# Weight sums in three stretches, each addition a round behind its copy; token tiles behind weight loads; two more gate buffers

## The chip, the cores and the metric

The kernel runs on one core of one Trainium2 chip. The metric is the device time of one launch in microseconds. The core has five engines with one instruction stream each (TensorE or PE, VectorE or DVE, ScalarE or ACT, GpSimd or POOL, SyncE or SP), and 16 DMA engines, to which here SP hands work through hardware queues and POOL through a software queue. Each stream runs in order: an instruction that waits holds back all that stands behind it on its engine.

## The reference

One step of a hybrid decoder layer over 1024 prompt tokens and 8 sample tokens, all in fp32. One input projection feeds two head groups, and one output projection joins them.

```python
p = project(rmsnorm(xp, norm_w[l]), w_in[l], b_igate[l], b_fgate[l])   # h @ w_in, split column-wise
att = dsa_prompt(p['q'], p['k'], p['v'], p['qi'], p['ki'], p['wi'])    # indexer scores, top-k keys, attention
h_ml, C1, n1, m1 = mlstm_run(p['mq'], p['mk'], p['mv'], p['ig'], p['lf'], zC, zn, zm, ML_CHUNK)
xp = merge(xp, att, p, h_ml, ml_norm_w[l], w_out[l])   # gates, then x + concat([a, mo]) @ w_out
# the sample tokens: the same with a paged cache (cache_k, cache_v, cache_idx_k) and given mLSTM states
```

The model width is 2048. The tokens are handled as 1032 columns (1024 and 8) in two halves of 516. This case turns on the wide columns of `w_in`: 40 tiles of 128 columns (the mLSTM q, k, v, its output gate and both SiLU gates).

## The kernel before

**Matmuls.** Each fp32 product is made of three matmuls on split operands. A raw tile is cast on ACT into a high part H, DVE subtracts H from the raw tile to leave a low part L, and PE adds H·H, H·L and L·H. A weight is used only after its load (SP), its cast (L262, or L1770 in the wide stage) and its subtraction (L263, or L1771).

**Stages on PE.** First come projection tiles 0 to 20 with the plain scheme (`proj`, matmuls at L1599), until about 522 us. Then `gate_stage` makes the 40 wide tiles in pairs by a seven-product scheme of the Strassen kind: of a pair of column tiles and the two token halves it forms sums of weight blocks and sums of token blocks, and needs fewer products for it. It has 140 products of 48 matmuls (L1782), until about 1607 us: first kinds 4 and 6 in turn (40 products, raw weights), then kind 1 (20), kind 3 (20), kind 2 (20), and at last kinds 0 and 7 in turn (40). The output projection (L2086 and L2153) follows.

**Weight sums.** Kinds 1, 3 and 2 read sums of two or more weight blocks, which lie in `usD[n, i]` in DRAM (n is the sum, i one of NP = 20 tile pairs; `b11` to `b22` are the four blocks of a pair). `job_usum` makes one sum of 512 KB by two DMAs: a copy of one block into place (`copy`, L1472 on SP for n = 0 and 3, L1474 on POOL for n = 1 and 2), and an accumulating DMA (`plus`, L1478 on POOL). There are 160 of these steps. A plus waits until its copy has landed, and so does a copy whose source is another sum.

**Token sums.** `xsD` holds sums of token tiles. `fill` (L1738) loads tiles of them, 258 KB each, into the buffers `xL` of a slot that a later kind reads; three ticks later they are split as weights are (L1731, L1733). A tick is half a product.

**Partial products.** PE's results go through DVE (`combine`, L1877) into buffers of 516 columns called `ev`, from there to DRAM (`put`, L1805, into `spD`), and are read back (`get`, L1801, from `spD` into an `ev` buffer) a product kind later. `outs` is the ring of four such buffers, which `get`, `put` and the gates share. `ones` are two buffers of that size, the halves of the tile `rstd`, which only the last stage uses after the reciprocal norms have been read from them.

**What sets the order.** A scheduler orders every engine's stream at build time by a simulation of the kernel; `tc.high_priority()` lets an instruction go ahead, `pin` keeps it in place, and `tc.issue_after(x)` puts it behind the instruction `x` on its queue. `pace["dma"]` is the last weight load that was written. Side jobs (indexer, attention on both token sets, mLSTM, the weight sums) run in three `Lane`s: each job has a first and a last time in units of a projection tile (T_AK = 9, T_G = 21 is the first wide tile, the wide stage goes to 61) and a number of steps, and its lane spreads the steps over that time. The lane of the sums runs beside the two others and gives its DMAs to the same SP and POOL streams. On POOL stand also the gathers of the paged index keys (`kp`, L1013, indirect DMAs), which feed matmuls on PE at L1035; the gathers for the sampled tokens' attention (`ck`, L1290); and on DVE that attention's products and sums (L1347, L1351). The selection of keys runs on ACT and DVE (L524, L548 to L553) and, for the sample tokens, through a count on PE (L1073) between DVE steps (L1069, L1090 to L1102).

Of the kernel before, what the change touches and what calls it, by code (L numbers as in the profile page):

```python
# [8 lines left out]
F32 = mybir.dt.float32  # L9
# [33 lines left out]
T_AK = 9  # L43
T_AV = 11
T_AQ = 13
T_G = 21
# [10 lines left out]
NP = (NT - T_G) // 2  # L57
# [120 lines left out]
def body(tc, A, stop=None):  # L178
    nc = tc.nc
    V, SC, G, PE, SY = nc.vector, nc.scalar, nc.gpsimd, nc.tensor, nc.sync  # L180
# [25 lines left out]
    early = ExitStack()  # L206
# [14 lines left out]
    pin = tc.keep_in_program_order  # L221
    pace = {}
# [5 lines left out]
    def dt_(shape, name):  # L228
        return tc.dram_tile(shape, F32, name=name)
# [15 lines left out]
    usD = dt_([4, NP, 128, 2, 4, 128], "usD")  # L245
# [1212 lines left out]
                yield 1  # L1458

    sums = set()  # L1460
    NE = 64

    def job_usum():
        def parts(i):
            c1 = T_G + 2 * i - 1
            return [[A["wa"][c, y] for y in range(2)] for c in (c1, c1 + 1)]

        def copy(n, i, src, queue):
            with tc.high_priority():
                if queue is SY:  # L1470
                    with tc.issue_after(pace["dma"]):
                        SY.dma_start(usD[n, i], src)  # L1472
                else:
                    pin(queue.dma_start(usD[n, i], src))  # L1474

        def plus(n, i, src):
            with tc.high_priority():
                pin(G.dma_start(usD[n, i], src, accum_op=OP.add, max_dma_last_dim=8192))  # L1478
            sums.add((n, i))

        for i in range(NP + 1):
            (b11, _), (b12, _) = parts(min(i, NP - 1))
            b22 = parts(i - 1)[1][1] if i else None
            if i < NP:
                copy(0, i, b11, SY)
                yield 1
            if i:
                copy(1, i - 1, usD[0, i - 1], G)
                yield 1
            if i < NP:  # L1490
                plus(0, i, b12)
                yield 1
            if i:
                plus(1, i - 1, b22)
                yield 1
        for n, src in ((3, None), (2, 1)):
            for i in range(NP):
                (_, b21), (b12, b22) = parts(i)
                copy(n, i, b22 if n == 3 else usD[1, i], SY if n == 3 else G)
                yield 1  # L1500
                plus(n, i, b12 if n == 3 else b21)
                yield 1

    def att_free():
        return "datt" in lanes[1].done and "k" in mlc
# [17 lines left out]

    groups = ((2, 3), (4, 5), (6, 7))

    def shares(gen, n):
        g = gen()

        def part(n):
            for _ in range(n):  # L1530
                w = next(g, 0)
                if not w:
                    return
                yield w
        return lambda: part(n), lambda: part(10 ** 6)

    sums_a, sums_b = shares(job_usum, NE)
    lanes = [Lane([Job("gates", 5, T_AK - 0.5, 12500, job_gates),
                   Job("index", T_AK + 1.5, 31.5, 6000 + sum(map(ix_weight, groups)), lambda: job_index(groups)),
                   Job("att", T_G + 17.6, 49.3, 2 * 2 * sum(2 * (1 + (i + 1) * 0.5) for i in range(8)) + 18, job_att, att_free),  # L1540
# [4 lines left out]
                   Job("qrows", T_G + 0.2, 27, 1, job_qrows),  # L1545
                   Job("datt", T_G + 9.2, 38.4, 10000 + 8 * 7000 + 34000 + 5 * 2500 + 8000 + 8000 + 5000, job_datt),
                   Job("dml", T_G + 20, 55.5, 28000 + 16 * 2500 + 5000, job_dml, hi_done)]),
             Lane([Job("early sums", T_AK + 2.5, 22.0, NE, sums_a),
                   Job("late sums", T_AK, 46.0, 8 * NP - NE, sums_b)])]
    gateV = gateS.rearrange("(k p) r -> k p r", p=128)  # L1550
    mixb = [None] * KT
    first = []
# [129 lines left out]
    def gate_stage():  # L1682
# [3 lines left out]
        raws, ones = [[one[:, 0], one[:, 1], one]], []  # L1686
        evs = evp.big["ev"].rearrange("p a b -> p (a b)")
        outs = [evs[:, x * HR:x * HR + HR].rearrange("p (c t) -> p c t", c=2) for x in range(4)]
        mlc["k"] = [X[:, 14:16, HR:HR + 512] for X in (XH, XL)]
        turn = {"raw": 0, "w": 0, "ev": 0, "one": 0, "n": 0}  # L1690
# [30 lines left out]
        def tick():  # L1721
            nonlocal pa0, pb0
            now = 4.0 * T_G + state["u"] * amount
            for lane in lanes:
                lane.step(now, amount)
            state["u"] += 1
            if splits and splits[0][0] <= state["u"]:
                _, h, l = splits.pop(0)
                with tc.high_priority():
                    with tc.issue_after(pace["act"]):  # L1730
                        SC.copy(h, l.bitcast(F32))  # L1731
                    with tc.issue_after(pace["dve"]):
                        V.tensor_tensor(l, l.bitcast(F32), h.bitcast(F32), OP.subtract)  # L1733
            if fills:
                f = fills.pop(0)
                if f:
                    h, l, src = f
                    SY.dma_start(l.bitcast(F32), src)  # L1738
                    splits.append((state["u"] + 3, h, l))
            if now >= 4.0 * T_PRE and pb0 is None:  # L1740
                lanes[0].ensure("ml")
                pb0 = mctx.enter_context(tc.tile_pool(name="pb0", bufs=1, side="right"))
            if now >= 4.0 * T_PA and pa0 is None:
                lanes[1].ensure("dml")
                pa0 = mctx.enter_context(tc.tile_pool(name="pa0", bufs=1, side="right"))
            while ready and ready[0][0] < state["u"] and (pb0 if ready[0][1] > 1 else pa0) is not None:
                pend.append(ready.pop(0)[1])
            for _ in range(2):
                if len(mids) > 4:
                    mixmake(*mids.pop(0), True)  # L1750
                if pend:
                    k = pend.pop(0)
                    mids.append(mixload(k, pb0 if k > 1 else pa0, True, G))
# [149 lines left out]
                mlc["lo"] = True  # L1903
        del extra, both
        ones += [rstd[:, c * HR:c * HR + HR].rearrange("p (c t) -> p c t", c=2) for c in range(2)]
        turn["p"] = 0

        def two():
            return [take("p", pj), take("p", pj)]
# [29 lines left out]
        def flush():  # L1939
            while muls:  # L1940
                times, ks = muls.pop(0)
                times()
                ready.extend((state["u"], k) for k in ks)
# [27 lines left out]
        def out_weight(q):  # L1971
            H, L, load, cast = wload(A["wo"][0, q], 128, wst, 2, 3)
            pin(load(slice(0, 4)))
            for x in cast(slice(0, 4)):
                pin(x)
            first.append((H, L))

        def last():
# [1 line left out]
            out_weight(2)  # L1980

        flush()
        for p in range(3):
            fetch(p)
        for p, (z, i, y) in enumerate(order):
# [9 lines left out]
            e, g = fetched.pop(p)  # L1995
# [93 lines left out]
    parts = [[(0, 0), (0, 1), (0, 2), (1, 0), (1, 1), (1, 2), (0, 3)], [(1, 3)]]  # L2089
# [38 lines left out]
    turn = [0]  # L2128
# [76 lines left out]
    late = []  # L2205
# [91 lines left out]
    for n in range(2):  # L2297
        p6, p4 = banks3(0), banks3(1)
        for k in range(8):
            with tc.high_priority():  # L2300
                b12 = wblock(0, 2 + n, k, pt, 6)
                b11 = wblock(0, n, k, pt, 6)
                b22 = wblock(1, 2 + n, k, pt, 6)
                b21 = wblock(1, n, k, wst, 2)
# [22 lines left out]
    for n in range(2):  # L2327
        ps = banks3(n)
        for k in range(8):
            with tc.high_priority():  # L2330
                b22 = wblock(1, 2 + n, k, pt, 6)
                b12 = wblock(0, 2 + n, k, *((wst, 2) if k % 2 else (pt, 6)))
# [133 lines left out]
```

## Time and profile before

| | us |
|---|---|
| median of 3 runs | 1963.96 (1962.99 to 1965.94) |
| the profiled run | 1964.0 |
| its span | 1962.2 |
| PE busy in it | 1895.3 |
| DVE busy | 1406.0 |
| ACT busy | 914.1 |
| POOL busy | 533.7 |

The profiled run is one execution, and the rows below come from it; what lies outside its span is 1.8 us. PE is busy for 97% of the span, so little is idle there (some 67 us). The questions are therefore where PE stands still, what it waits for there, and at which clock it runs next to these places. A row of the timeline gives the start, the duration, the engine, the line, the operation and its tiles, and in brackets the idle time before it with what ended that time. A row of the waits gives the total, the number of times and the longest. A row of the windows gives each engine's busy time in a stretch, then the granted clock of PE, the busy share of the DMA engines and the GB/s they moved.

### The profile page before, as it was taken

The page shows a single profiled execution, that of the slowest core. Times are in us where ns is not written, and L with a number is a line of the kernel's source. Part 1 is how long each engine was busy: PE and PEld are TensorE (multiplying, and loading weights), DVE is VectorE, ACT ScalarE, POOL GpSimd, SP SyncE. Part 2 cuts the span into 40 slices and gives each one's busy share as a digit, 9 for nine tenths or more (in the row PEclk, how much of TensorE's full clock was granted, in tenths as well). Part 3 has the DMA queues.
Part 4 walks back from the last instruction along what each step waited for, and adds up shares of the span by engine and source line. Part 5 has one row for each costly group of instructions (what it writes and reads, how often), then busy time and mean ns, then how long its engine had stood idle before and what let it go on. Part 6 is the DMA issues. An engine that isn't in the chain of part 4 may idle for free. (4 is left out here: it accounts for less than half of the span.)

```text
span 1962.2 us, 37412 instructions
## 1 busy us (share of the span) xinstructions
PE 1895.3 (97%) x13422; PEld 1820.9 (93%) x13422; DVE 1406.0 (72%) x3261; ACT 914.1 (47%) x1826; POOL 533.7 (27%) x614
## 2 busy tenths in 40 slices
PE   9999998999989999998899999999999989999997
PEld 9999998999979999998799999999999989977776
DVE  8554664767789985897465566657979866787797
ACT  8222252334543557621245565454656634454645
POOL 0599853321100001035111000001211340107632
PEclk9999998999989999999999999999999999999999
DMA  7577767879878759979998874458988778898866
GB/s 258 158 233 217 236 203 223 246 210 228 242 227 246 197 166 270 339 244 266 310 304 239 243 214 143 133 177 294 328 286 294 222 192 269 273 339 300 277 200 220
DMA packets 252918, 474.46 MB, mean 242 GB/s; under 512 B 40549, under 2 KB 116133, under 8 KB 246333
## 3 DMA queue, kind: packets, MB, share of 16 engines
q1 hardware_dynamic: 217261, 356.70, 55.8%
q0 software_dynamic: 21504, 107.32, 21.9%
q10 hardware_dynamic: 13968, 8.06, 1.4%
q8 instruction: 105, 1.72, 0.4%
q14 instruction: 80, 0.66, 0.1%
HBM read 381.54 MB, written 174.32 MB: 283 GB/s over the span
## 5 line engine op out<-in xcount | busy, mean ns | idle before, releaser
L1782 PE MATMUL pj<-xH 128*128 128x258 f32 x1920 | 548.2, 286 | 21.4 <-DVE ev L1877 14.1
L1782 PE MATMUL pj<-xL,xH 128*128 128x258 f32 x1920 | 548.2, 286 | 0.0
L1782 PE MATMUL pj<-xH,xL 128*128 128x258 f32 x1920 | 547.2, 286 | 0.0
L1782 PEld LDWEIGHTS pj<-xH 128*128 128x128 f32 x1920 | 365.2, 190 | 25.3 <-DVE ev L1877 15.3
L1782 PEld LDWEIGHTS pj<-xL,xH 128*128 128x128 f32 x1920 | 365.6, 190 | 2.4 <-issue 0.8
L1782 PEld LDWEIGHTS pj<-xH,xL 128*128 128x128 f32 x1920 | 365.4, 191 | 1.7
L1599 PE MATMUL pj<-xH,wH 128*128 128x344 f32 (+1 forms) x816 | 265.0, 328 | 1.9 <-DVE ev L385 1.1
L1599 PE MATMUL pj<-xL,wH 128*128 128x344 f32 (+1 forms) x816 | 266.2, 326 | 0.0
L1599 PE MATMUL pj<-xH,wL 128*128 128x344 f32 (+1 forms) x816 | 265.4, 326 | 0.0
L263 DVE TENSOR_TENSOR wL<-wraw,wH 128x512 fp32r<-128x512 f32 (+2 forms) x151 | 117.4, 789 | 106.2 <-ACT wH L262 99.9
L1478 POOL DMA_DIRECT2D usD<-in_wa_dram x80 | 66.5, 863 | 428.4 <-DMA usD<-in_wa_dram 228.8
L262 ACT CAST wH<-wraw 128x512 fp32r<-128x512 f32 (+2 forms) x151 | 89.8, 607 | 199.9 <-PE pj L1599 98.3
L1599 PEld LDWEIGHTS pj<-xH,wH 128*128 128x128 f32 x816 | 153.9, 189 | 3.6 <-DVE ev L385 1.8
L1599 PEld LDWEIGHTS pj<-xL,wH 128*128 128x128 f32 x816 | 154.1, 189 | 0.6 <-DVE xL L320 0.3
L1599 PEld LDWEIGHTS pj<-xH,wL 128*128 128x128 f32 x816 | 154.2, 189 | 0.4 <-DVE wL L263 0.3
L1770 ACT CAST xH<-wL 128x1024 fp32r<-128x1024 f32 (+1 forms) x91 | 76.1, 836 | 125.5 <-PE pj L1782 69.8
L1770 ACT CAST xH<-wH 128x1024 fp32r<-128x1024 f32 x91 | 76.0, 836 | 124.4 <-PE pj L1782 72.9
L2153 PE MATMUL pj<-wH,sH 128*128 128x512 f32 x336 | 131.3, 391 | 1.7 <-ACT wH L2137 1.7
L2153 PE MATMUL pj<-wH,sL 128*128 128x512 f32 x336 | 130.7, 390 | 0.0
L2153 PE MATMUL pj<-wL,sH 128*128 128x512 f32 x336 | 125.9, 393 | 4.8 <-DVE wL L2142 4.8
L477 ACT ACTIVATE rl<-bank 128x512 f32<-128x512 f32 (+2 forms) x160 | 79.8, 523 | 99.7 <-PE bank L475 55.1
L480 DVE SCALAR_TENSOR_TENSOR s<-rl,wiN,s 128x512 f32<-128x512 f32 (+2 forms) x150 | 106.6, 729 | 19.5 <-ACT rl L477 16.6
(492 smaller groups left out, 4507.4 us busy)
## 6 DMA issues: line engine op xcount, KB each, us to landing
usD<-in_wa_dram POOLq DMA_DIRECT2D x80, 512.0 KB, 7.8
wraw<-in_wt_dram SPq DMA_DIRECT2D x144, 256.0 KB
usD<-in_wa_dram SPq DMA_DIRECT2D x40, 512.0 KB
usD<-usD POOLq DMA_DIRECT2D x40, 512.0 KB, 7.2
wraw<-in_wa_dram SPq DMA_DIRECT2D x78, 256.0 KB
wraw<-in_wo_dram SPq DMA_DIRECT2D x64, 256.0 KB
ev<-spD SPq DMA_DIRECT2D x62, 258.0 KB
spD<-ev SPq DMA_DIRECT2D x60, 258.0 KB
```

Source lines behind the costliest of these rows:

```text
L262: a = SC.copy(H[:, s, :cols], raw[:, s, :cols])
L263: return a, V.tensor_tensor(L[:, s, :cols], raw[:, s, :cols], H[:, s, :cols].bitcast(F32), OP.subtract)
L477: SC.activation(r[:, :cn], p[:, :cn], AF.Relu)
L480: v = V.scalar_tensor_tensor(s[:, c0:c0 + cn], r[:, :cn], wv, s[:, c0:c0 + cn], OP.mult, OP.add)
L1478: pin(G.dma_start(usD[n, i], src, accum_op=OP.add, max_dma_last_dim=8192))
L1599: m = PE.matmul(ps[:cols, :cn], w_[:, k, :cols], x_[kk][:, c0:c0 + cn], start=(kk == ends[0] and z == 0), stop=(kk == ends[1] and z == 2))
L1770: paced("act", SC.copy(H[:, q], r))
L1782: PE.matmul(ps[c], w_[:, q, ks], x[y][:, c * CS:c * CS + CS], start=(first and q == 0 and k == 0 and z == 0), stop=(q == 1 and k == 3 and ...
L2153: PE.matmul(ps[b], S_[x][:, b * 128:b * 128 + 128], T_[y], start=(k == 0 and z == 0), stop=(k == 7 and z == 2))
```

## The change

1. `job_usum` writes each addition a round behind its copy. For n = 0 and 1 a round is now copy(0, i), copy(1, i-2), plus(0, i-1), plus(1, i-3); before, it was copy(0, i), copy(1, i-1), plus(0, i), plus(1, i-1). For n = 3 and 2 it is copy(i), plus(i-1); before, copy(i), plus(i).
2. The sums run in three stretches, not two. Before: 64 steps from tile 11.5 to 22, and 96 from there to 46. Now: 56 steps from tile 11.5 to 20.4, 62 from 22.4 to 33.2, and the last 42 from 38.8 to 47.
3. The loads of token sums (`xL<-xsD`) are queued behind the last weight load that was written before them.
4. The two halves of `rstd` join the ring of `ev` buffers for the 60 products of kinds 1, 3 and 2: six buffers in place of four. They leave it ahead of the last 40 products.
5. The casts of the first output weight get high priority.

```diff
-    NE = 64
+    NE, NF = 56, 62
...
-        for i in range(NP + 1):
-            (b11, _), (b12, _) = parts(min(i, NP - 1))
-            b22 = parts(i - 1)[1][1] if i else None
+        for i in range(NP + 3):
             if i < NP:
-                copy(0, i, b11, SY)
+                copy(0, i, parts(i)[0][0], SY)
                 yield 1
-            if i:
-                copy(1, i - 1, usD[0, i - 1], G)
+            if 2 <= i < NP + 2:
+                copy(1, i - 2, usD[0, i - 2], G)
                 yield 1
-            if i < NP:
-                plus(0, i, b12)
+            if 1 <= i <= NP:
+                plus(0, i - 1, parts(i - 1)[1][0])
                 yield 1
-            if i:
-                plus(1, i - 1, b22)
+            if i >= 3:
+                plus(1, i - 3, parts(i - 3)[1][1])
                 yield 1
-        for n, src in ((3, None), (2, 1)):
-            for i in range(NP):
-                (_, b21), (b12, b22) = parts(i)
-                copy(n, i, b22 if n == 3 else usD[1, i], SY if n == 3 else G)
-                yield 1
-                plus(n, i, b12 if n == 3 else b21)
-                yield 1
+        for n in (3, 2):
+            for i in range(NP + 1):
+                if i < NP:
+                    copy(n, i, parts(i)[1][1] if n == 3 else usD[1, i], SY if n == 3 else G)
+                    yield 1
+                if i:
+                    (_, b21), (b12, _) = parts(i - 1)
+                    plus(n, i - 1, b12 if n == 3 else b21)
+                    yield 1
...
-             Lane([Job("early sums", T_AK + 2.5, 22.0, NE, sums_a),
-                   Job("late sums", T_AK, 46.0, 8 * NP - NE, sums_b)])]
+             Lane([Job("early sums", T_AK + 2.5, 20.4, NE, lambda: share(adds, NE)),
+                   Job("middle sums", T_G + 1.4, 33.2, NF, lambda: share(adds, NF)),
+                   Job("late sums", T_G + 17.8, 47.0, 8 * NP - NE - NF, lambda: share(adds, 8 * NP))])]
...
-                    SY.dma_start(l.bitcast(F32), src)
+                    with tc.issue_after(pace["dma"]):
+                        SY.dma_start(l.bitcast(F32), src)
...
+        outs += ones
         turn["p"] = 0
+        turn["ev"] = 4
...
-            for x in cast(slice(0, 4)):
-                pin(x)
+            with tc.high_priority():
+                for x in cast(slice(0, 4)):
+                    pin(x)
...
         flush()
+        del outs[4:]
```

The same instructions are issued on every engine. What moves stands in three places. Each listing gives a stream in order, a row as line, operation, tiles and shape, with "x4" for four like it in a row. The lines of the changed kernel are two lower here (L1767 for L1769, L1736 for L1738, L1799 for L1801, L1803 for L1805).

SP at the start of the wide stage (about 515 to 545 us), before. `wraw`, `wH` and `wL` at L1769 are the wide weights; `aqS` is the stored query projection.

```order
L1769 DMA wraw<-in_wa_dram 128x1024
L1472 DMA usD<-in_wa_dram 16x8192
L1738 DMA xL<-xsD 128x516 x4
L1769 DMA wraw<-in_wa_dram 128x1024
L1472 DMA usD<-in_wa_dram 16x8192
L416 DMA aqS_104<-ev 128x344 x2
L1738 DMA xL<-xsD 128x516
L1769 DMA wH<-in_wa_dram 128x1024
L1769 DMA wL<-in_wa_dram 128x1024
L1769 DMA wH<-in_wa_dram 128x512
L1769 DMA wL<-in_wa_dram 128x512
```

And now:

```order
L1767 DMA wraw<-in_wa_dram 128x1024 x2
L416 DMA aqS_104<-ev 128x344 x2
L1767 DMA wH<-in_wa_dram 128x1024
L1767 DMA wH<-in_wa_dram 128x512
L1767 DMA wL<-in_wa_dram 128x1024
L1767 DMA wL<-in_wa_dram 128x512
L416 DMA aqS_104<-ev 128x336
L1803 DMA spD<-ev 128x516
```

The sums and the eight early token loads are gone from between the first wide weights; the token loads now stand further back, one at a time between weight loads.

SP some 400 us later, in kind 3 (about 930 to 945 us), before. The row `sn<-in_sn_dram` marks the same place in both.

```order
L1801 DMA ev<-spD 128x516
L1185 DMA gi<-gD 128x64
L1805 DMA spD<-ev 128x516
L1187 DMA bb<-in_bg_dram 128x8
L1189 DMA sn<-in_sn_dram 128x32
L1191 DMA m_14327<-in_sm_dram 128x32
L1769 DMA wH<-usD 128x1024
L1801 DMA ev<-spD 128x516
L1805 DMA spD<-ev 128x516
L1738 DMA xL<-xsD 128x516 x3
L1769 DMA wL<-usD 128x1024
```

And now:

```order
L1736 DMA xL<-xsD 128x516
L1799 DMA ev<-spD 128x516
L1803 DMA spD<-ev 128x516
L1767 DMA wL<-usD 128x1024
L1736 DMA xL<-xsD 128x516
L1799 DMA ev<-spD 128x516
L1296 DMA qb<-qrowS 128x1024
L1767 DMA wH<-usD 128x512
L1803 DMA spD<-ev 128x516
L1767 DMA wL<-usD 128x512
L1736 DMA xL<-xsD 128x516
L1799 DMA ev<-spD 128x516
```

The token loads stand singly where three or more stood together; a read-back `ev<-spD` keeps its place between a weight load and a put.

POOL at the first index-key gathers (about 280 to 312 us), before:

```order
L1474 DMA usD<-usD 16x8192
L1478 DMA usD<-in_wa_dram 64x2048 x2
L1013 DMA kp<-in_cik_dram,idx 128x512 x2
L1474 DMA usD<-usD 16x8192
L1478 DMA usD<-in_wa_dram 64x2048 x2
L1013 DMA kp<-in_cik_dram,idx 128x512 x3
```

And now:

```order
L1474 DMA usD<-usD 16x8192
L1478 DMA usD<-in_wa_dram 64x2048
L1013 DMA kp<-in_cik_dram,idx 128x512 x2
L1474 DMA usD<-usD 16x8192
L1478 DMA usD<-in_wa_dram 64x2048 x2
L1013 DMA kp<-in_cik_dram,idx 128x512 x2
L1474 DMA usD<-usD 16x8192
L1013 DMA kp<-in_cik_dram,idx 128x512
```

Ahead of the first pair of gathers stands one addition fewer; between the first pair and the next stand a copy and two additions, as before. The second of these two now belongs to a copy of the round before.

On PE the matmuls of the gathered keys (L1035) come a little earlier: before, 234 matmuls of a projection tile, 8 of the keys, 41, 4; now 202, 4, 13, 4, 42, 8. From about 1310 us on, all streams are in the same order in both kernels, the first output weight's casts among them.

More of the change, by code (lines that the diff above doesn't have):

```diff
@@ L1524, in body, with share @@
     groups = ((2, 3), (4, 5), (6, 7))
[L1526 to L1537, printed above, removed]
+    def share(gen, n):
+        for _ in range(n):
+            w = next(gen, 0)
+            if not w:
+                return
+            yield w
+    adds = job_usum()
     lanes = [Lane([Job("gates", 5, T_AK - 0.5, 12500, job_gates),
```

## The prediction

> **What bounds the kernel now.** I read the busy times first, then the waits of PE, then the timeline of PE at the longest of them, the windows for the clock beside them, and last SP, POOL and DVE just ahead of each gap.
>
> ```profile
> PE 1895.3 (97%) x13422; PEld 1820.9 (93%) x13422; DVE 1406.0 (72%) x3261; ACT 914.1 (47%) x1826; POOL 533.7 (27%) x614
> ...
> PE pj L1782 <- DVE ev L1877: 14.1, 6, 4.6
> PE bank L1035 <- DMA kp<-in_cik_dram,idx: 7.6, 2, 7.5
> PE pj L1782 <- DVE im L552: 5.2, 1, 5.2
> PE bank L1073 <- DVE cb L1069: 4.0, 1, 4.0
> PE bank L604 <- DMA wL<-usD: 3.1, 1, 3.1
> PE pj L1782 <- DVE im L1100: 2.2, 1, 2.2
> ```
>
> PE sets the time: 1962.2 - 1895.3 = 66.9 us of idle time is all that can be won without taking matmuls away, and these six waits are 36.2 of it. They lie in three places:
>
> ```profile
> 314.86 0.58 PE L1035 MATMUL bank<-bd,kp 128*128 128x128 f32 x1 [7.48 <-DMA kp<-in_cik_dram,idx]
> ...
> 547.74 0.55 PE L1782 MATMUL pj<-xH 128*128 128x258 f32 x1 [5.15 <-DVE im L552]
> ...
> 557.13 0.20 PE L1073 MATMUL bank<-cb,onesb 128*128 128x24 bf16 x1 [3.99 <-DVE cb L1069]
> ...
> 927.24 0.58 PE L1782 MATMUL pj<-xH 128*128 128x258 f32 x1 [4.40 <-DVE ev L1877]
> ...
> 945.16 0.45 PE L1782 MATMUL pj<-xH 128*128 128x258 f32 x1 [4.61 <-DVE ev L1877]
> ...
> 967.58 0.39 PE L1782 MATMUL pj<-xH 128*128 128x258 f32 x1 [2.98 <-DVE ev L1877]
> ...
> 988.01 0.63 PE L604 MATMUL bank<-cst,pP 128*128 128x128 f32 x4 [3.08 <-DMA wL<-usD]
> ```
>
> The first is the index-key gathers, the second the start of the wide stage, the third kind 3. Beside the long gaps PE also runs slower; in the windows the figure ahead of the DMA share is the granted clock:
>
> ```profile
> 315.00:320.00 5.00, 5.00 (x21) 5.00 (x22) 0.77 (x2) 0.05 (x1) 1.06 (x1) 0.50 1.04 317
> 925.00:930.00 5.00, 2.76 (x13) 2.76 (x14) 4.02 (x7) 1.64 (x3) 1.97 (x2) 0.50 0.73 256
> 930.00:935.00 5.00, 5.00 (x36) 4.80 (x36) 5.00 (x7) 0.12 (x1) 3.53 (x4) 0.83 0.78 159
> 965.00:970.00 5.00, 2.42 (x20) 2.42 (x21) 2.90 (x5) 0.00 (x0) 1.29 (x2) 1.00 0.94 331
> ```
>
> After the gap of 7.48 us PE works 5 us at half the clock, which loses 2.5 us; after that of 4.40 it loses 2.76 x 0.50 + 5.00 x 0.17 = 2.2 us; after that of 2.98 nothing. So a gap of 4 us or more costs its length and about 2 us, a shorter one its length. The Trainium skill ("TensorE: Matmul & The Clock Gate", Part 1: The HAM clock gate) has the clock fall to half after an idle window of about 3.4 us and come back after as much work; the trace agrees, with 2.98 us on one side and 4.40 on the other.
>
> **Part by part: the start of the wide stage.** SP's and ACT's rows ahead of the gap at 547.74, and the window around it:
>
> ```profile
> 515.31 2.03 SPq L1738 DMA_DIRECT2D xL<-xsD  x4
> ...
> 529.71 1.05 ACT L1770 CAST xH<-wraw 128x1024 fp32r<-128x1024 f32 x1 [6.03 <-DMA wraw<-in_wa_dram]
> ...
> 536.36 1.93 SPq L1738 DMA_DIRECT2D xL<-xsD  x3
> ...
> 541.78 0.62 ACT L1770 CAST xH<-wH 128x512 fp32r<-128x512 f32 x1 [4.31 <-DMA wH<-in_wa_dram]
> ...
> 515.00:563.00 48.00, 36.36 (x246) 35.45 (x244) 35.46 (x120) 17.86 (x33) 6.27 (x9) 0.86 0.92 282
> ```
>
> ACT has nothing to cast for 6.03 and then 4.31 us, because the wide weights land late; PE's gap of 5.15 us ends 6 us behind the second cast, through the subtraction and the DVE steps ahead of it, and that of 2.2 us stands in the same way to the first. At that time the DMA engines are 92% busy, and SP gives them eight token loads and three copies of sums. The first token load is cast only at 622.6 us (row below), 100 us later: it is early for nothing. The change takes these loads and copies away from here (parts 2 and 3), and the weights stand directly behind each other. The two gaps are 2.2 + 5.15, and the half clock behind the second costs about 2 by the rows above: 9.4 us. DVE has 35.46 us of work in the 48, PE 36.36, so DVE does not forbid it. The gap at 557.13 is a chain on DVE (L1090 to L1069) between two counts on PE that stand next to each other in both orders; it stays. I take -8, with -6 (the first weight still lands late) and -9.4 as ends.
>
> **Kind 3.** SP's rows ahead of the gaps, DVE's wait from 900 to 990 us, the additions in 900 to 1000 us, and two windows:
>
> ```profile
> 906.91 0.38 SPq L1805 DMA_DIRECT2D spD<-ev  x1
> 916.12 0.32 SPq L1801 DMA_DIRECT2D ev<-spD  x1
> ...
> 918.47 0.40 SPq L1769 DMA_DIRECT2D wL<-usD  x1
> 928.06 0.32 SPq L1801 DMA_DIRECT2D ev<-spD  x1
> ...
> DVE ev L1877 <- DMA ev<-spD: 8.3, 2, 5.7
> ...
> L1478 POOL DMA_DIRECT2D usD<-in_wa_dram x10: 773/794/961, 906.1 to 996.0; - x10
> L1474 POOL DMA_DIRECT2D usD<-usD x9: 556/753/777, 920.2 to 996.6; - x9
> ...
> 900.00:950.00 50.00, 40.40 (x301) 39.37 (x299) 28.54 (x45) 8.13 (x14) 26.15 (x27) 0.90 0.91 284
> 950.00:1000.00 50.00, 42.02 (x334) 38.38 (x333) 24.40 (x57) 12.93 (x19) 6.44 (x10) 1.00 1.04 318
> ```
>
> SP stands still from 907.3 to 916.1 and from 918.9 to 928.1, each time ahead of a read-back `ev<-spD`. A read-back needs a free buffer of the four: it waits for the put of an older partial product, which waits for PE, and behind it on SP wait the weight loads that PE needs. So a late product makes the next weights late. With two more buffers (part 4) the read-back goes when the slot before last is free, and SP is no longer tied to PE at this place. In addition 19 sums run here beside the weights, at a DMA share of 1.04. The new stretches put no sum between tile 33.2 and 38.8 (about 818 to 940 us by the rows of this run); behind that, 42 steps over 8.2 tiles. A wide tile takes (1607 - 522) / 40 = 27 us by the ends of the stage, so that is 42 / 222 = 0.19 a us, as now. And the token loads come one by one. The gaps named are 4.40 + 4.61 + 2.98 + 3.08 = 15.1; with the short ones beside them PE is idle for 100 - 40.40 - 42.02 = 17.6; the clock costs 2.2 behind the first and some 2 behind the second: about 21.8. The gaps behind 950 us fall in a stretch whose sums stay as dense, so I count the first two with their clock in full, 4.4 + 4.6 + 4.2 = 13.2, and of the rest 1: -14. Ends: -8, if the sampled tokens' attention on DVE holds the rest; -22, if all goes.
>
> **The index-key gathers.** POOL's rows, and its waits for copies over the whole run:
>
> ```profile
> 305.40 0.87 POOL L1478 DMA_DIRECT2D usD<-in_wa_dram x1 [10.72 <-DMA usD<-usD]
> 306.57 1.06 POOL L1013 DMA_INDIRECT kp<-in_cik_dram,idx  x1 [0.31 <-issue]
> ...
> POOL usD L1478 <- DMA usD<-usD: 185.6, 28, 10.7
> ```
>
> The third gather is issued at 306.57, behind an addition that waited 10.72 us for its own copy; PE gets its data at 314.86, 8.3 us later. In the new order the addition belongs to an older copy and waits for nothing here, so the gather can be issued about 10 us earlier. But ahead of it in the software queue stand the same copy and two additions, of 512 KB each. Before, the queue took 8.3 us for an addition of 512 KB and a gather of 256 KB behind it, 768 KB. Now the copy, two additions and the gather are 1792 KB, from about 305.40 - 10.72 = 294.7 on: 294.7 + 8.3 x 1792 / 768 = 314, where it ended before. PE now wants the first keys 32 matmuls earlier and those of the second pair together, so its wait begins no later, and can come in two pieces. I count +2. Ends: -8, if the earlier issue counts in full (7.48 and most of the 2.5 at half clock), and +5, if the first pair is waited for as well. The Trainium skill ("DMA: Bandwidth & Descriptors", Queues, rings and completion order) has the descriptors of one ring consumed in ring order, which speaks for the +2; no row quoted here shows a gather overtake a sum, nor settles it. By that rule alone the gain of part 1 at this place would be nothing.
>
> POOL's 28 waits for copies, 185.6 us in all, become shorter by part 1, but of what stands behind them PE waits only for these gathers; elsewhere they are worth nothing to PE.
>
> **What the change adds elsewhere.** The casts of the token loads, the sums between 563 and 818 us, and two windows:
>
> ```profile
> L1731 ACT CAST xH<-xL x40: 614/618/627, 622.6 to 1216.0; 128x516 fp32r<-128x516 f32 x40
> ...
>   DMA xL<-xsD: 2.2, 1
> ...
> L1478 POOL DMA_DIRECT2D usD<-in_wa_dram x21 | 16.6, 862 | 199.6 <-DMA usD<-in_wa_dram 179.3 <-issue 14.0 <-DMA usD<-usD 6.2
> ...
> 563.00:818.00 255.00, 254.80 (x2023) 249.14 (x2024) 211.75 (x534) 140.23 (x232) 20.64 (x26) 1.00 0.81 234
> 750.00:800.00 50.00, 50.00 (x419) 50.00 (x418) 33.47 (x100) 37.95 (x63) 8.68 (x10) 1.00 1.00 304
> ```
>
> The middle stretch has 62 steps where now 21 additions run with about as many copies, 42: 20 more of 0.52 MB, which is 41 GB/s over 255 us. At the rate of these rows (234 GB/s at a share of 0.81) that is a share of 0.14 more, 0.95 in all. At a share of 1.00 in 750 to 800 us PE was busy for 50.0 of 50 us, so I cost it at 0. Its cover is that the weights run two to three products ahead; without it the price is a gap of 4.4 and a clock loss of 2.2 at a time.
>
> The token loads keep their casts (from 622.6 us on). Behind each of them on SP there is still a weight load whose cast stands ahead of the tokens' cast on ACT, so they can hardly be waited for where the weights are not: 0, at worst the 2.2 of the row, twice. The two halves of `rstd` as buffers: nothing else reads them then, 0. The output weight's casts keep their places in the order: 0.
>
> **The sum.** -8 - 14 + 2 = -20. The profiled run took 1964.0 us (1962.2 and 1.8 around it), which is the median. The forecast is 1944 us.
>
> **The rivals.** *The gathers come free as well.* POOL's wait of 10.72 us speaks for it, the queue ahead of them against it. Then -8 - 14 - 8 = -30 and 1934; with the whole of kind 3 it would be 1964 - 8 - 22 - 8 = 1926. I give it 0.2.
>
> *The waits only change their name.* Between 550 and 600 us and in kind 3 DVE has its own chains (the 3.99 us at L1069; the 8.3 us that DVE waits in two pieces for read-backs may be short because PE was late too). If half the gaps come back as waits for DVE or for a put, as when the ring was not what held SP, it is -4 - 7 + 2 = -9: 1955. I give it 0.2.
>
> *Slower: the middle stretch starves the weights.* 62 sums come in 255 us; in the start of the wide stage a share of 0.92 was enough to make weights late by 4 to 6 us. Each such gap costs 4.4 + 2.2 = 6.6. Three of them take the gain of 20; the fourth makes it slower, 1944 + 26 = 1970, and six give 1984. Against it speaks that 750 to 800 us passes at 1.00 without a gap, where the loads were as crowded. I give it 0.08.
>
> *It doesn't do what it says.* If the earlier places in the order free nothing, because each weight load waits for its buffer and not for SP, the time stays within 4 us: 0.05.
>
> **How the numbers follow.** The forecast has 0.47. Its own range is -6 - 8 + 5 = -9 to -9.4 - 22 + 2 = -29: 1935 to 1955. With the first rival (1926 to 1934) below and the second (1955) above, 1929 to 1959 leaves out about 0.2. A measurement of this kernel tells a difference from about 0.2%, 3.9 us. Faster by more than that: 0.47 + 0.2 + the most of 0.2 = 0.85. The rest of the second and the fourth make 0.07 for no change, the third 0.08 for slower.
>
> **What would show it.** In the changed kernel's timeline, PE's gap with `im L552` near 547 us is gone or under 2 us, ACT's waits of 6.03 and 4.31 us for wide weights with it; SP no longer stands still for 9 us ahead of `ev<-spD`, and PE's waits for DVE `ev` fall from 14.1 us to under 5; PE still waits some 7 to 10 us for `kp`; the windows from 563 to 818 us show PE at 99% or more at a share near 0.95. The forecast is wrong if PE waits there for weights, if the wait for `kp` goes, or if the waits in kind 3 return under L1351, L1371 or L1073.

## The result, and the profile after

The changed kernel takes 1991.4 us (median of 4 runs) where the kernel before takes 1963.5: a ratio of 1.0143, 95% interval 1.0107 to 1.0178. It is slower by 28 us; 20 us faster were forecast, with 1959 as the upper end of the range. The profiled run took 1989.0 us, its span 1987.2, which is 25 us more than before.

First the busy times and the longest waits of PE after the change:

```profile
PE 1897.8 (96%) x13422; PEld 1819.6 (92%) x13422; DVE 1406.0 (71%) x3261; ACT 916.1 (46%) x1826; POOL 533.5 (27%) x614
...
PE pj L1780 <- DVE rstd L1875: 20.1, 4, 9.5
PE bank L604 <- DMA pP<-avS: 16.2, 3, 13.0
...
PE bank L1073 <- DVE cb L1069: 5.3, 3, 4.0
PE bank L1035 <- DVE bd L1030: 2.6, 1, 2.6
PE bank L1035 <- DMA kp<-in_cik_dram,idx: 2.3, 2, 1.4
```

The wait for the key gathers has shrunk from 7.6 to 2.3 us, and `im L552` (5.2 us) is gone from the list. In their place stand two that are longer than any before: up to 9.5 us at a time for DVE's step on a partial product (`rstd` is one of the two new buffers), and 13.0 us for a load of the prompt attention. The windows, with PE's busy time first among the engines, and clock, DMA share and GB/s at the end, say where. Those of the kernel before that were not shown above:

```profile
300.00:350.00 50.00, 41.72 (x268) 40.97 (x267) 23.95 (x69) 11.31 (x27) 20.55 (x22) 0.90 0.85 239
500.00:550.00 50.00, 42.62 (x301) 41.81 (x300) 36.12 (x124) 24.06 (x45) 4.96 (x7) 0.96 0.89 276
550.00:600.00 50.00, 45.54 (x351) 45.05 (x350) 44.81 (x148) 19.70 (x34) 4.97 (x7) 0.90 0.78 224
1000.00:1050.00 50.00, 50.00 (x396) 48.83 (x395) 31.75 (x78) 28.52 (x63) 6.44 (x10) 1.00 0.92 265
1050.00:1100.00 50.00, 50.00 (x398) 48.75 (x397) 30.27 (x85) 26.76 (x64) 7.71 (x12) 1.00 0.88 239
```

Those of the changed kernel:

```profile
300.00:350.00 50.00, 45.17 (x314) 44.32 (x313) 28.20 (x86) 13.99 (x32) 21.10 (x23) 1.00 0.85 255
500.00:550.00 50.00, 44.70 (x327) 43.76 (x327) 44.14 (x152) 25.17 (x47) 4.23 (x6) 0.97 0.74 199
550.00:600.00 50.00, 49.16 (x412) 48.79 (x411) 46.80 (x141) 16.45 (x26) 5.79 (x8) 1.00 0.88 252
563.00:818.00 255.00, 251.34 (x1981) 245.75 (x1980) 206.70 (x522) 141.24 (x230) 23.49 (x29) 0.99 0.87 256
900.00:950.00 50.00, 43.05 (x317) 38.54 (x317) 28.53 (x57) 9.99 (x16) 20.85 (x26) 0.90 0.96 286
950.00:1000.00 50.00, 29.48 (x210) 28.84 (x210) 11.00 (x20) 6.48 (x9) 11.57 (x18) 0.81 1.03 308
1000.00:1050.00 50.00, 34.28 (x228) 32.52 (x228) 20.66 (x45) 14.56 (x28) 5.44 (x8) 0.78 0.99 311
1050.00:1100.00 50.00, 50.00 (x397) 48.98 (x396) 30.79 (x83) 27.38 (x64) 0.00 (x0) 1.00 0.40 120
```

Up to 600 us the changed kernel is ahead. At the gathers PE idles 3.4 us less (50 - 41.72 before, 50 - 45.17 now) and keeps its clock. At the start of the wide stage (500 to 600 us) it idles 6.1 us where it idled 100 - 42.62 - 45.54 = 11.8. The middle stretch has one new gap of 3.7 us. All is lost between 900 and 1050 us: PE idles 43.2 us there, against 9.6 + 7.98 + 0 = 17.6 before, and the half clock takes about 29.48 x 0.19 + 34.28 x 0.22 = 13 us more of the last two windows. The DMA share is 1.03 while this goes on, and falls to 0.40 right behind it, where it was 0.88 before: the same work has been pressed into a shorter time. Two rows of PE's timeline there:

```profile
980.98 0.58 PE L1780 MATMUL pj<-xH 128*128 128x258 f32 x1 [9.49 <-DVE rstd L1875]
...
1015.73 1.09 PE L604 MATMUL bank<-cst,pP 128*128 128x128 f32 x4 [12.97 <-DMA pP<-avS]
```

The first row names the step on the partial product, but that is only the last link. ACT's and DVE's rows just ahead of it:

```profile
979.25 0.62 ACT L1768 CAST xH<-wH 128x512 fp32r<-128x512 f32 x1 [9.17 <-DMA wH<-usD]
...
979.90 0.69 DVE L1769 TENSOR_TENSOR xL<-wH,xH 128x512 fp32r<-128x512 f32 x1 [8.48 <-ACT xH L1768]
980.51 0.75 DVE L1875 TENSOR_TENSOR rstd<-pj,rstd 128x258 f32<-128x258 f32 x2
```

DVE's step at 980.51 stood behind the subtraction of a weight, which waited for its cast, and the cast had waited 9.17 us for the weight to land. PE's gaps of 6.30 us (to 963.72) and 4.73 us (to 999.16) end in the same way, behind casts that had waited 13.39 and 13.79 us. So what came late were loads: of weights three times, and of the prompt attention.

The work is that of the sums for n = 2. POOL's copies and additions from 900 to 1300 us, with the first and last start, before:

```profile
L1478 POOL DMA_DIRECT2D usD<-in_wa_dram x22: 773/784/961, 906.1 to 1101.2; - x22
L1474 POOL DMA_DIRECT2D usD<-usD x20: 556/758/777, 920.2 to 1092.5; - x20
...
  DMA usD<-usD: 147.9, 20
```

And after:

```profile
L1478 POOL DMA_DIRECT2D usD<-in_wa_dram x22: 781/787/1212, 912.8 to 1022.1; - x22
L1474 POOL DMA_DIRECT2D usD<-usD x20: 637/752/1179, 914.0 to 1012.2; - x20
...
  DMA usD<-usD: 82.3, 19
```

A round of one copy and one addition took (1092.5 - 920.2) / 19 = 9.1 us, and now takes (1012.2 - 914.0) / 19 = 5.2. POOL waited 148 us for copies in this time, and now waits 82. Between these rounds stands nothing else on POOL: neither a matmul nor a weight load holds them. So what had set their pace was the wait of each addition for its own copy. Part 1 of the change lets an addition run beside the next copy, and only the smaller wait for the copy of the round before is left.

### The profile page after: what moved, and what is told of

The parts are those of the page before. It is cut to its first block, busy times and chain, and to the rows that moved or that the text cites. A ratio compares the mean times of both kernels' runs of the same rounds, so it can differ in the third digit from the quotient of the medians.

```text
span 1987.2 us, 37383 instructions
## 1 busy us (share of the span) xinstructions
PE 1897.8 (96%) x13422; PEld 1819.6 (92%) x13422; DVE 1406.0 (71%) x3261; ACT 916.1 (46%) x1826; POOL 533.5 (27%) x614
## 5 line engine op out<-in xcount | busy, mean ns | idle before, releaser
L1780 PE MATMUL pj<-xH 128*128 128x258 f32 x1920 | 550.8, 287 | 28.5 <-DVE rstd L1875 20.1
L1769 DVE TENSOR_TENSOR xL<-wH,xH 128x1024 fp32r<-128x1024 f32 x91 | 87.2, 959 | 49.5 <-ACT xH L1768 49.3
```

Source lines behind the costliest of these rows:

```text
L1769: paced("dve", V.tensor_tensor(L[:, q], r, H[:, q].bitcast(F32), OP.subtract))
L1780: PE.matmul(ps[c], w_[:, q, ks], x[y][:, c * CS:c * CS + CS], start=(first and q == 0 and k == 0 and z == 0), stop=(q == 1 and k == 3 and ...
```

## The experiments

In all of them ratios are taken against runs of the kernel before on the same chip; the runs of one kernel lie up to 1% apart there, so a ratio and its interval say more than a single time.

### First: what holds the sums, what stretches and ring do

**Pairs for n = 2.** The changed kernel with each addition directly behind its copy for n = 2 alone:

```diff
-        for n in (3, 2):
-            for i in range(NP + 1):
...
+        for i in range(NP + 1):
+            if i < NP:
+                copy(3, i, parts(i)[1][1], SY)
+                yield 1
+            if i:
+                plus(3, i - 1, parts(i - 1)[1][0])
+                yield 1
+        for i in range(NP):
+            copy(2, i, usD[1, i], G)
+            yield 1
+            plus(2, i, parts(i)[0][1])
+            yield 1
```

> The changed kernel with one thing undone: for n = 2 each addition stands directly behind its own copy again, as before; all else stays. In the changed kernel POOL ran the 20 rounds of n = 2 from 913 to 1022 us (5.2 us a round, DMA share 1.03 from 950 to 1000), before from 906 to 1101 us. Theory A (the wait of each addition for its own copy was what held the sums back; without it they take the DMA engines from the weight loads): the rounds take 9 to 11 us again, to about 1100 us, PE is busy for over 46 us in each of the windows 950:1000 and 1000:1050, and the time falls to 1945 to 1955. Theory B (the three stretches are the cause, since the sums of n = 2 start no earlier than 912 us whatever their order): the time stays at 1985 or more. Theory C (the ring of six and the single token loads hold SP): it stays at 1985 or more, with SP still waiting 10 us and more ahead of read-backs.

Measured: 1955.4 us, 0.9932 (0.9909 to 0.9956). Its sums, and its windows:

```profile
L1474 POOL DMA_DIRECT2D usD<-usD x20: 767/776/1176, 925.2 to 1095.6; - x20
...
950.00:1000.00 50.00, 40.91 (x308) 39.95 (x307) 21.85 (x46) 13.59 (x25) 6.45 (x10) 0.90 1.02 320
1000.00:1050.00 50.00, 50.00 (x392) 48.62 (x391) 32.42 (x84) 27.90 (x64) 7.71 (x12) 1.00 0.91 258
```

A round takes 9.0 us again, the time is just above the upper end that theory A gave (1955), and from 1000 to 1100 us PE is busy all the time. One gap of 9.1 us (a load of the prompt attention) is left in 950 to 1000, so PE's time there is 40.9 us and not over 46 as theory A had it. This one edit is worth 2.1% of the time, and theories B and C fall: stretches and ring were left as changed.

**Two stretches.** The changed kernel with the lane of before:

```diff
-             Lane([Job("early sums", T_AK + 2.5, 20.4, NE, lambda: share(adds, NE)),
-                   Job("middle sums", T_G + 1.4, 33.2, NF, lambda: share(adds, NF)),
-                   Job("late sums", T_G + 17.8, 47.0, 8 * NP - NE - NF, lambda: share(adds, 8 * NP))])]
+             Lane([Job("early sums", T_AK + 2.5, 22.0, 64, lambda: share(adds, 64)),
+                   Job("late sums", T_AK, 46.0, 96, lambda: share(adds, 8 * NP))])]
```

> The changed kernel with the two stretches of before (64 steps to tile 22, 96 to tile 46), but still each addition a round behind its copy, the token loads behind weight loads and six buffers. Theory A: POOL is not held by its own waits, so n = 2 still comes in a bunch of about 5 us a round as soon as POOL is through with the gathers ahead of it, and the time stays at 1980 or more. Theory B: the time falls below 1960.

Measured: 2006.0 us, 1.0205 (1.0161 to 1.0249). So the stretches don't cause the loss; without them it is no smaller (the interval overlaps a little with the changed kernel's, 1.0107 to 1.0178).

**Four buffers.** The changed kernel with the ring of before:

```diff
-        outs += ones
...
-        turn["ev"] = 4
...
-        del outs[4:]
```

> The changed kernel with four buffers in the ring, as before. Theory A: no gain from this, 1985 to 2010, since the bunch of sums stays and SP waits the more with fewer buffers. Theory C: below 1970.

Measured: 2001.3 us, 1.0149 (1.0113 to 1.0184), which the interval doesn't tell from the changed kernel's 1.0143. Theory C falls, and the ring can neither be blamed nor credited.

**Copies of n = 2 on SP.** The additions stay a round behind:

```diff
-                    copy(n, i, parts(i)[1][1] if n == 3 else usD[1, i], SY if n == 3 else G)
+                    copy(n, i, parts(i)[1][1] if n == 3 else usD[1, i], SY)
```

> The changed kernel with the copies of n = 2 issued by SP behind the last weight load, as those of n = 0 and 3 are, and not by POOL; the additions stay on POOL, a round behind. Theory A: the copies now come at the pace of the weight loads, so the sums spread from about 940 to 1200 us at 8 to 12 us a round, the gaps of 955 to 1021 us go, and the time is 1940 to 1955, as good as with the pairs of the other run or better. Theory B: they still start late, and kind 2 or kind 3 waits for them: 1975 or more.

Measured: 1957.2 us, 0.9951 (0.9921 to 0.998). Its copies:

```profile
L1472 SPq DMA_DIRECT2D usD<-usD x20: 473/474/1063, 917.4 to 1144.9; - x20
```

That is (1144.9 - 917.4) / 19 = 12 us a round, and PE is busy for the whole of 950 to 1050 us. The time is just above the 1940 to 1955 that theory A gave, and no better than with the pairs (0.9932). The order "a round behind" does no harm once something else sets the pace. What harmed was the loss of that pace.

### Second: each part alone

**Part 1 alone.** The kernel before, with the rounds of `job_usum` from the change (its core):

```diff
-            if i:
-                copy(1, i - 1, usD[0, i - 1], G)
+            if 2 <= i < NP + 2:
+                copy(1, i - 2, usD[0, i - 2], G)
...
-            if i < NP:
-                plus(0, i, b12)
+            if 1 <= i <= NP:
+                plus(0, i - 1, parts(i - 1)[1][0])
...
-                plus(n, i, b12 if n == 3 else b21)
+                    plus(n, i - 1, b12 if n == 3 else b21)
```

> The kernel before with one thing changed: each addition a round behind its copy (part 1), in the two stretches of before, with four buffers and early token loads. Theory A (the lost wait of POOL lets the sums of n = 2 come in a bunch): the 20 rounds of n = 2 take about 110 us in place of 195, PE loses 20 us and more in 950 to 1050 us, and the time is 1.01 to 1.03 of before. Rival: part 1 harms only together with the late third stretch; then it is 0.99 to 1.00.

Measured: 2005.3 us, 1.0201 (1.0163 to 1.0239).

```profile
L1474 POOL DMA_DIRECT2D usD<-usD x20: 556/756/887, 917.8 to 1011.7; - x20
...
950.00:1000.00 50.00, 22.57 (x137) 18.54 (x138) 9.23 (x25) 4.91 (x7) 12.88 (x20) 0.64 1.03 314
```

A round takes 4.9 us, and PE works for 22.6 of the 50 us at 0.64 of its clock. Part 1 does its harm by itself.

**Part 3 alone.** The kernel before, with:

```diff
-                    SY.dma_start(l.bitcast(F32), src)
+                    with tc.issue_after(pace["dma"]):
+                        SY.dma_start(l.bitcast(F32), src)
```

> The kernel before with the token loads queued behind weight loads (part 3) and nothing else. The prediction's term for the start of the wide stage (-8) came from the token loads and the sums together; if the token loads carry it, PE's gaps of 2.2 and 5.15 us near 533 and 547 us go with this part alone and the time is 0.994 to 0.997 of before; if the sums carry it, they stay, and the time is within 0.2%.

Measured: 1964.7 us, 0.9992 (0.9969 to 1.0015). PE is busy for 44.27 + 44.86 = 89.1 us between 500 and 600, against 88.2 before: the token loads alone free hardly anything. ACT still waits for the first wide weights:

```profile
528.19 1.05 ACT L1771 CAST xH<-wraw 128x1024 fp32r<-128x1024 f32 x1 [4.58 <-DMA wraw<-in_wa_dram]
...
534.17 1.05 ACT L1771 CAST xH<-wH 128x1024 fp32r<-128x1024 f32 x1 [4.93 <-DMA wH<-in_wa_dram]
```

Where the gap of 5.15 us stood, PE has one of 4.15 us (to 546.37), now under the name of a partial product.

**Part 4 alone.** The kernel before, with:

```diff
+        outs += ones
...
+        turn["ev"] = 4
...
+        del outs[4:]
```

> The kernel before with six buffers in the ring for kinds 1, 3 and 2 (part 4) and nothing else. The prediction had SP's stops of 9 us ahead of read-backs at 907 and 919 us come from the ring of four. If so, these stops and PE's gaps of 4.40 and 4.61 us go, and the time is 0.992 to 0.996 of before. If SP stood there because the products themselves were late, the stops stay and the time is within 0.3%.

Measured: 1967.4 us, 1.0009 (0.9988 to 1.003). SP's rows at the stops:

```profile
911.38 0.38 SPq L1805 DMA_DIRECT2D spD<-ev  x1
911.81 0.80 SPq L1296 DMA_DIRECT2D qb<-qrowS  x1
920.32 0.32 SPq L1801 DMA_DIRECT2D ev<-spD  x1
...
922.60 0.42 SPq L1805 DMA_DIRECT2D spD<-ev  x1
923.11 0.38 SPq L1769 DMA_DIRECT2D wL<-usD  x1
933.28 0.32 SPq L1801 DMA_DIRECT2D ev<-spD  x1
```

The stops of 8 and 10 us are still there. In SP's stream the read-back stands one or two rows behind a put, and these stops end when just that put has landed, in this kernel as in the one before. SP's waits from 890 to 1060 us:

```profile
SPq L1801 <- DMA spD<-ev: 49.0, 12, 9.7
SPq L1801 <- DMA spD<-rstd: 28.1, 7, 5.1
```

That is 77.1 us of waiting for puts, where the kernel before has 84.1 in the same time. So such a stop is the landing time of a 258 KB put in a crowded time (8.9 and 10.7 us here), and the two further buffers hardly change it. Presumably the scheduler with six buffers only draws each read-back forward until it stands close behind the put of the buffer that it takes; no run tests that.

**All but part 1.** The changed kernel with the rounds of `job_usum` of before, for all four sums:

```diff
-                copy(1, i - 2, usD[0, i - 2], G)
+                copy(1, i - 1, usD[0, i - 1], G)
...
-                plus(0, i - 1, parts(i - 1)[1][0])
+                plus(0, i, b12)
...
-                    plus(n, i - 1, b12 if n == 3 else b21)
+                plus(n, i, b12 if n == 3 else b21)
```

> The changed kernel with the rounds of before (each addition directly behind its own copy, for all four sums), but the three stretches, six buffers and the late token loads. Theory A: POOL is held by its own waits again and the time is 0.990 to 0.998 of before, as with the pairs for n = 2 alone; the difference to that run is what part 1 is worth for n = 0, 1 and 3 (the index-key gathers), and is within 5 us. Rival: part 1 for n = 0 and 1 is what helped near 300 to 350 us, and without it the time is 1965 or more.

Measured: 1954.5 us, 0.9936 (0.9915 to 0.9958). Beside the 0.9932 of the pairs for n = 2, part 1 is worth nothing for n = 0, 1 and 3. Both beat the kernel before.

### Third: where the gain is, and one thing beside the change

**Part 2 alone.** The kernel before, with (the core of it):

```diff
-    NE = 64
+    NE, NF = 56, 62
...
-             Lane([Job("early sums", T_AK + 2.5, 22.0, NE, sums_a),
-                   Job("late sums", T_AK, 46.0, 8 * NP - NE, sums_b)])]
+             Lane([Job("early sums", T_AK + 2.5, 20.4, NE, lambda: share(adds, NE)),
+                   Job("middle sums", T_G + 1.4, 33.2, NF, lambda: share(adds, NF)),
+                   Job("late sums", T_G + 17.8, 47.0, 8 * NP - NE - NF, lambda: share(adds, 8 * NP))])]
```

> The kernel before with the three stretches (part 2) and nothing else: old rounds, four buffers, early token loads. All but part 1 together gave 0.9936; the token loads alone gave 0.9992 and the ring alone 1.0009, so if the parts add up, the stretches alone give 0.993 to 0.996 (no sums between about 500 and 560 us and between 820 and 915 us). Rival: the parts help only together (the sums gone and the token loads single); then it is 0.998 to 1.001.

Measured: 1956.1 us, 0.9954 (0.9935 to 0.9973). This is most of the gain. ACT's waits for the first wide weights are gone here (the longest wait for a load that is left there is 0.72 us), and with them both gaps of PE near 533 and 547 us.

**Parts 2 and 3.** The kernel of the run above, with the token loads late as well:

```diff
+                    with tc.issue_after(pace["dma"]):
+                        SY.dma_start(l.bitcast(F32), src)
```

> The kernel before with the three stretches and the late token loads, but four buffers and old rounds. If the ring is worth nothing also here, 0.992 to 0.996, the same as all but part 1 (0.9936). If the ring helps once the DMA engines are freer, 0.996 or more.

Measured: 1954.6 us, 0.994 (0.9915 to 0.9965). Between 500 and 600 us PE is now busy for 45.40 + 47.39 = 92.8 us, against 90.7 with the stretches alone and 89.1 with the token loads alone. These are single profiles (the one with the stretches alone is of its slowest run, 1966.5 us), and all but part 1, which has both, shows 44.85 + 46.89 = 91.7; so it isn't shown that the token loads add anything, here or in the ratio (0.9954 and 0.994). The ring, and the high priority of part 5, bring nothing that these intervals can show (0.9936 with both).

**The load of small pieces on ACT's queue.** In the pairs kernel, and in the runs with four buffers and with copies on SP, PE waited 9.5 to 11.0 us, in gaps that end at 321 to 323 us. The row names `bd`, a product of DVE for the gathered keys, but this stood behind the subtraction of a late weight, so PE waited for weights in place of keys. (With part 1 and two stretches it waited for keys as before, up to 6.1 and 8.3 us.) The rows of the pairs kernel:

```profile
318.54 0.62 ACT L262 CAST wH<-wraw 128x512 fp32r<-128x512 f32 x1 [15.93 <-DMA wraw<-in_wa_dram]
...
319.19 0.69 DVE L263 TENSOR_TENSOR wL<-wraw,wH 128x512 fp32r<-128x512 f32 x1 [13.53 <-ACT wH L262]
...
321.57 1.06 DVE L1030 TENSOR_TENSOR bd<-iqr,g 128x512 f32<-128x512 f32 x1
...
322.68 0.58 PE L1035 MATMUL bank<-bd,kp 128*128 128x128 f32 x1 [9.69 <-DVE bd L1030]
```

And SP's rows ahead of them:

```profile
292.55 0.68 SPq L1003 DMA_DIRECT2D wib<-miscS  x1
295.48 14.52 SPq L259 DMA_DIRECT2D wraw<-in_wa_dram  x2
```

SP needed 14.5 us to issue two weight loads behind `wib`, which is made of 2048 pieces of 32 bytes. So the pairs kernel was run with this load on ACT's queue, and all but part 1 likewise:

```diff
-            SY.dma_start(wib, miscS[64:80, S:R].partition_broadcast(128))
+            SC.dma_start(wib, miscS[64:80, S:R].partition_broadcast(128))
```

> The changed kernel with pairs for n = 2 (0.9932 in an earlier run) and one load moved from SP to ACT's queue: wib, 2048 pieces of 32 bytes, behind which the two next weight loads of SP take 6 us in the kernel before and 10 to 14 us in the changed one and its variants to issue. Theory: these small pieces fill the queue that the weight loads share; moved away, the two issues take under 2 us, PE's wait of 9.7 us near 313 to 322 us goes, and the time is 0.987 to 0.991 of before. Rival: the pieces crowd the DMA engines themselves, wherever they are queued: no change, 0.992 to 0.995.

Measured: 1957.9 us, 0.9961 (0.9938 to 0.9984). Its profiled run took 1946.3 us, and shows:

```profile
295.36 4.55 SPq L259 DMA_DIRECT2D wraw<-in_wa_dram  x2
...
300.00:350.00 50.00, 50.00 (x347) 49.84 (x347) 32.40 (x103) 16.42 (x39) 23.50 (x25) 0.99 0.91 278
```

In that execution the two issues take 4.6 us, not the expected 2 or less, and PE is busy for all of 300 to 350 us (a gap of 2.8 us ends ahead of it, at 298.09, at the first keys); in the pairs kernel it was busy for 40.31 us there. Yet the median of its 12 runs is no better than without it (0.9932). The expected 0.987 to 0.991 did not come, and why a gap of 9.7 us that is gone in the profile doesn't show in the median stays open: the runs lie between 1945 and 1964 us, and only one of them has a profile.

> All but part 1 (0.9936 in an earlier run) with wib on ACT's queue. The gathers of index keys stand behind POOL's waits again, so PE still waits some 7 us for kp near 311 us, and the gain over 0.9936 is at most 3 us: 0.991 to 0.994. Against the run beside it this shows what part 1 is worth at the gathers once the weights come in time: 4 to 8 us if POOL's wait was what held kp, nothing if the software queue was.

Measured: 1951.7 us, 0.9932 (0.9911 to 0.9953), the lowest median of all, but not to be told from the 0.9936 without it. PE waited 3.3 us for keys, not 7. The comparison with the run beside it speaks against any worth of part 1 at the gathers, if for anything: 0.9961 with it, 0.9932 without.

## Why the prediction was wrong, step by step

**Kind 3 (-14 forecast).** This is the step that failed, in the sentence "that is 42 / 222 = 0.19 a us, as now". Measured are 42 sums in 109 us, 0.38 a us, twice that. I took the first and last tile of a lane's job for the time in which its DMAs run. They set only where the DMAs stand in the stream; how fast POOL goes through the stream is decided by what stands between them, and here nothing did but the waits for copies. The same text had these waits in hand ("POOL's 28 waits for copies, 185.6 us in all") and set them to nothing, since PE waits for little behind them. They were worth a lot: they spread the sums. Taking them away alone costs 2.0%, giving them back for n = 2 alone brings 2.1%. In place of -14 the step came to about +39 us in the changed kernel's profile: 25.6 of idle time and 13 of clock between 900 and 1050 us. PE's waits for DVE's steps on partial products, which were to fall from 14.1 us to under 5, rose to 26.4 (20.1 under `rstd`, 6.3 under `ev`).

**The ring.** "A read-back needs a free buffer of the four" was right as a rule of the program, but the conclusion that two more buffers let SP go was wrong, shown by the part alone: SP waits for the put that stands close ahead of it.

**The start of the wide stage (-8).** Right. The gap with `im L552` is gone, and so are ACT's waits for wide weights; 5.7 us of idle time and some 4 us of clock (0.90 before and 1.00 now in 550 to 600 us) are saved, and the chain between the two counts kept its 3.99 us. But the mechanism was only half right: the stretches alone take ACT's waits and both gaps away, the late token loads alone do not, so by these profiles it was the sums that made the weights late, and the eight token loads had little part in it.

**The gathers (+2).** The landing by the software queue was put at 314 us; in the changed kernel the keys of the first two gathers were used at 291.7 and 294.6 us, and those of the third landed at 303.1, for which PE waited 0.8 us. POOL's rows of it:

```profile
284.52 1.27 POOL L1013 DMA_INDIRECT kp<-in_cik_dram,idx  x1 [13.54 <-DVE idx L1006]
...
287.10 0.57 POOL L1474 DMA_DIRECT2D usD<-usD  x1
287.66 1.77 POOL L1478 DMA_DIRECT2D usD<-in_wa_dram  x2
289.74 1.06 POOL L1013 DMA_INDIRECT kp<-in_cik_dram,idx  x1 [0.30 <-issue]
```

This execution reached the gathers 6 us earlier (284.52, before 290.61), and the copy and the two additions ahead of the third gather went through with it in 16 us (287.1 to 303.1), not 19.4. So the size of the term was wrong, and its sign: in this profile the place won 3.4 us of idle time and some 4 us of clock (0.90 before, 1.00 now), which is what the first rival had. But the gain is not a lasting one: in the pairs kernel, with the same POOL order up to these gathers, weights were late in place of keys and PE was busy for 40.31 us of 300 to 350, less than before. Over all runs part 1 shows no worth here (0.9936 without it, 0.9932 with it for n = 0, 1 and 3), so the times don't bear the first rival out either.

**The middle stretch (0).** Nearly right: a share of 0.87 and not 0.95, PE at 98.6% and not 99, with one gap of 3.7 us. The third rival named the right mechanism, sums that starve the weights and cost gaps with half clock behind them, but placed it here, where 22 of 24 copies are on SP behind weight loads and keep the pace; it came at the stretch whose copies are on POOL. Its chance of 0.08 was too small for that reason: it was weighed at one place only.

**The sum.** The steps add up to what the changed kernel's profile shows: +39 in kind 3, +3.7 in the middle stretch, about -8 at the gathers and -10 at the start of the wide stage make about +25, and its span is 25 us longer. Without part 1 the change brings 0.64%, which is 12.6 us of the 20 forecast. The second rival, gaps that come back under other names, has its share in the rest: in the pairs kernel PE waits 9.1 us in 950 to 1000 us for a load of the prompt attention, a wait that the list of before doesn't have; in all but part 1 it is 9.9 us.

## What to carry to other kernels

A wait that costs its own engine time can be the only thing that sets the pace of a background transfer: before it is taken away, ask what holds the transfer back instead, and read the pace from starts in the trace, not from the span that a planner gives it. If a copy and its addition are to overlap, tie their issue to something that moves with the work (here the weight loads on SP), as the run with the copies on SP did, though here that was no faster than leaving each addition behind its copy (0.9951 against 0.9932). And before a ring is made larger, look which transfer the waiting one waits for: here it was a put just issued, and two more buffers brought nothing.

## What the runs showed that was not expected

SP's issue of two weight loads behind the load of 2048 pieces of 32 bytes took 6.0, 5.7, 7.4, 5.7, 7.3 and 6.9 us in the six profiles with old rounds and this load on SP, and 11.3, 14.5, 11.1, 10.6, 10.4 and 10.4 us in the six where additions stand a round behind their copies. An issue on SP's queue thus took longer where part 1 had changed the order on POOL's (10.4 us with part 1 alone, 6.0 before); it is only the profiles, one of each kernel, that show it, and the cause inside the queues is not shown. Nor are the small pieces shown to be the cause: with their load on ACT's queue the issue fell to 4.6 us in the pairs kernel, but in all but part 1 it took 5.8 us with the move and 5.7 without.

The crowded time fell on the loads that PE needed and not on the sums: from 950 to 1000 us, at a share of 1.03, the rounds of sums ran at 5 us while PE was idle for 20 of 50 us. From 900 to 1050 us ACT waited 63.5 us for weights (`wH` and `wL` from `usD`) in the changed kernel, 48.1 before and 31.4 in the pairs kernel.
